# First FFN of a two-layer encoder step: parts of x shared between the opening's plain products and the seven operands, and the first chunk's down products by seven

## The chip, the cores and the metric

The kernel runs on one core of a Trainium2 chip. The engines of the core work in parallel and are tied together by semaphores: PE (matmul), DVE (vector work), ACT (scalar-engine copies and functions), POOL, and SP, which issues loads. The metric is the device time of one execution in microseconds; before the change the median of three runs is 2510.49 us (2510.39 to 2510.75). In this text "width" is the number of elements per partition: 128x320 is 128 partitions of 320.

## The reference

One inference step of an encoder trunk with two layers, 640 tokens in all (512 of a prompt, 8 times 16 of running streams), model width 1024, inner FFN width 2816, all in fp32.

```python
for l in range(DEPTH):                                  # DEPTH = 2
    x = x + 0.5 * _swiglu(_rmsnorm(x, norm_ffn1[l]), w_ffn1_gu[l], w_ffn1_down[l])
    x = x + mixer(_rmsnorm(x, norm_mix[l]))             # short conv + band attention, gated
    x = x + 0.5 * _swiglu(_rmsnorm(x, norm_ffn2[l]), w_ffn2_gu[l], w_ffn2_down[l])
y = _rmsnorm(x, norm_final)

def _swiglu(h, w_gu, w_down):
    g, u = jnp.split(h @ w_gu, 2, axis=-1)
    return (jax.nn.silu(g) * u) @ w_down
```

(Shortened: the reference carries prompt and streams separately and returns keys, values and convolution states too.) The change lies in the first FFN of the first layer.

## The kernel before, in words

**Layout.** x is held transposed: eight tiles x[0..7] of 128 model columns by T = 640 tokens. A block of a weight matrix is 128x128. Tokens are cut into two halves t1 and t2 of HT = 320, since one matmul writes 320 wide.

**Three matmuls for one product.** Every operand is split into a high part (fp32r, the copy on ACT) and a low part (the rest, a subtraction on DVE, `split`, `flush`, `low`). A product of weight w and operand x is wh·xh + wh·xl + wl·xh: three matmuls for each half of the tokens. Weights arrive in raw slabs of 128x1024 (eight blocks), loaded by SP, and are split by `prep` (ACT, line 320) and `flush` (DVE, line 325) into whi and wlo, three buffers each.

**Plain and by seven.** A plain product (`multiply`, `product`) goes over both halves of the tokens: for two blocks of rows of the weight, two of x and two halves of tokens that is eight block products. By seven (`gate_up`, `down_rows`) the same 2x2x2 is done with seven block products, whose operands are sums: of the weights four (X's partners 65, 6, ... built on DVE by `source` from the raw slabs with `add`, line 264) and of x or of the activations also four. In the code the seven operands of x are named X11, X21, X22, XT5, XN6, XT7, XT4; E holds the even tile's sums, O the odd one's. The name `ex.ops[kp]` is a pair of tiles (hi, lo) of seven parts each, for x's tiles 2kp and 2kp + 1. Four partial sums a, b, c are kept in PSUM and copied out by ACT in between (c1, u2, c5; lines 779 to 798 and 832 to 848), since PE goes on adding into the same bank: PE's next product into a bank waits for the copy.

**The FFN** (`ffn`) takes its 22 blocks of inner width in chunks, for the first FFN 4, 4, 4, 4, 4, 2. For a chunk it makes gate and up products (`gate_up`, by seven, one call for each block), and between them the down products of the chunk before: plain, "down", two of x's tiles at a time with `pd` as PSUM tile; or by seven, "rows", four tiles at a time (`down_rows`, PSUM tiles `d..`), which `by_seven` decides. In a rows block DVE adds four of the partial sums for each two tiles straight into x (`take`, line 991), and ACT's copies of the others are added by transfers that POOL issues (`send`, line 986). `Pair` makes the seven operands of two activations for the latter, `later` and `TURNS` say at which places of the following work its sums are made.

**The opening** (`opening`) is the first chunk of the first FFN. x is not normalised yet, so its four gates and ups are made plainly from x times the norm's gain, product after product (PSUM tiles `po`, 0 to 7) with slab i for product i, while x's squares, the norm and then, by `ex.final`, the seven operands of x for later chunks are made between. The scale of the norm, rho, is multiplied in afterwards. At its end the four activations u are split by `parts`, run as `tails` in the first `gate_up` that follows (branch `first`, block 4). The four plain down pieces of this chunk follow gate/ups 4, 5, 6 and 7.

**Order.** In this stretch the order on PE, DVE and ACT is the one in which the code records the work (`ORDERED`); from block 6 on (`free`) only PE's is, and the others are placed by a scheduler.

```python
def by_seven(name, j):
    at, n = chunk_at(name, j)
    return n == 4 and at >= FFNS[name][1] and at + n < FT
```

FFNS["a0"][1] is 4, the number of blocks of the opening.

Of the kernel before, what the change touches and what calls it, by code (L numbers as in the profile page):

```python
# [22 lines left out]
T = SEQ + NB * TS  # L23
HT = T // 2
# [6 lines left out]
KT = D // P  # L31
FT = FF // P
# [8 lines left out]
NP = KT // 2  # L41
# [18 lines left out]
XT4, XN6, XT7, X21, X22, X11, XT5 = range(7)  # L60
# [123 lines left out]
def halves(t):  # L184
    return t.rearrange("p (a b) -> p a b", a=2)
# [3 lines left out]
def trunk(ctx: ExitStack, tc: tile.TileContext, xin, wst, small, pbias, samplebias, kcache, vcache,  # L189
# [36 lines left out]
    def split(hi, lo, src):  # L226
        ACT.copy(hi, src)
        DVE.tensor_tensor(out=lo, in0=src, in1=hi.bitcast(F32), op=ALU.subtract)
# [31 lines left out]
            SP.dma_start(raw, wst[n])  # L260
        return raws[i]

    def add(out, a, b):
        DVE.tensor_tensor(out=out, in0=a, in1=b, op=ALU.add)  # L264

    h1, h2 = slice(0, CH // 2), slice(CH // 2, CH)
    whole = slice(0, CH)
# [55 lines left out]
    def flush():  # L323
        for lo, src, hi in pending:
            DVE.tensor_tensor(out=lo, in0=src, in1=hi.bitcast(F32), op=ALU.subtract)  # L325
        pending.clear()
# [20 lines left out]
    def begin():  # L347

        prep(used[0] + 2)
# [33 lines left out]
    def multiply(ps, ws, xs, first, last):  # L383
        (wh, wl), (xh, xl) = ws, xs
        for j, (w, x) in enumerate(((wh, xh), (wh, xl), (wl, xh))):
            for a in range(2):
                PE.matmul(ps[:, a, :HT], w, x[:, a * HT : (a + 1) * HT],  # L387
                          start=first and j == 0, stop=last and j == 2)

    def steps(ps, ops, at=()):  # L390
# [32 lines left out]
    POOL.memset(epst, EPS)  # L423
    early = cp.tile([P, 1], F32, name="early")

    less = cp.tile([P, L * KT], F32, name="less")
    POOL.tensor_scalar(out=less, in0=sm[:, O_GM : O_GM + L * KT], scalar1=-1.0, scalar2=None, op0=ALU.mult)

    x = [xp.tile([P, T], F32, name=f"x{k}") for k in range(KT)]
    for k in range(KT):  # L430
# [73 lines left out]
    class Expand(Stats):  # L504
# [12 lines left out]
        def final(self, m, square=True):  # L517
# [46 lines left out]
            elif not end:  # L564
                self.add()

        def flush(self):
            for lo, src, hi in self.late:
                DVE.tensor_tensor(out=lo, in0=src, in1=hi.bitcast(F32), op=ALU.subtract)
            self.late.clear()  # L570
# [42 lines left out]
            ACT.activation(early, epst, AF.Silu)  # L613
            self.known = True

    def opening(fp, name, goff, n, put, tails):

        ACT.copy(early, epst)  # L620
        ex = Expand(fp, name, goff)
        h = []
        whi, wlo = (wp.tile([P, CH], F32R, tag=f"w{t}", name=f"w{t}0", bufs=3) for t in ("hi", "lo"))
        ready.append((whi, wlo))
        for k in range(KT):
            g = sm[:, goff + k : goff + k + 1]
            hi = hp.tile([P, T], F32R, tag="hhi", name=f"hhi{name}_{k}")
            lo = hp.tile([P, T], F32R, tag="hlo", name=f"hlo{name}_{k}")
            ACT.activation(hi, x[k], AF.Copy, scale=g)
            c = slice(k * P, (k + 2) * P)  # L630
            if k % 2 == 0:
                ACT.copy(whi[:, c], raws[0][:, c])
            DVE.scalar_tensor_tensor(out=lo, in0=x[k], scalar=g, in1=hi.bitcast(F32),
                                     op0=ALU.mult, op1=ALU.subtract)
            if k % 2 == 0:
                DVE.tensor_tensor(out=wlo[:, c], in0=raws[0][:, c], in1=whi[:, c].bitcast(F32),
                                  op=ALU.subtract)
            h.append((hi, lo))
        flush()

        made = {2: (0, 1), 3: (2, 3), 4: (4,), 5: (5, 6), 6: (7,)}
        us, gs, ps = [], [], []

        def out(i):

            j, up = divmod(i, 2)
            if not up:
                gs.append(tmp(f"g{name}_{j}"))
                if j:
                    scaled(gs[j], ps[i], ex.rho)  # L650
                    ACT.activation(gs[j], gs[j], AF.Silu)
                else:
                    ACT.copy(halves(gs[j]), two(ps[i]))
                return
            u = tmp(f"u{name}_{j}") if j > 1 else fp.tile([P, T], F32, tag="cap", name=f"u{name}_{j}", bufs=5)
            us.append(u)
            if j:
                scaled(u, ps[i], ex.rho)
                DVE.tensor_tensor(out=u, in0=u, in1=gs[j], op=ALU.mult)
# [36 lines left out]
        ahead()  # L696
        begin()
        out(2 * n - 1)

        def parts(j, u):  # L700
            hi = hp.tile([P, T], F32R, tag="hhi", name=f"ahi{name}_{j}")
            lo = hp.tile([P, T], F32R, tag="hlo", name=f"alo{name}_{j}")
            split(hi, lo, u)
            put(j, (hi, lo))
# [179 lines left out]
    class Pair:  # L884
# [8 lines left out]
        def product(self, n, u, g, hi, lo):  # L893
# [15 lines left out]
            self.low(halves(lo), halves(hi), z[:, at])  # L909
            self.keep(kinds, hi, lo)  # L910

        def low(self, lo, hi, z):
            DVE.tensor_tensor(out=lo, in0=z, in1=hi.bitcast(F32), op=ALU.subtract)

# [116 lines left out]
    def ffn(name, fp, ex, goff, after, end=False):  # L1031
# [7 lines left out]
        hold[0] = True  # L1039

        mode = ExitStack()
        free = min(j for j in range(FT) if by_seven(name, j)) + 2

        def order(engines):
            mode.close()
# [1 line left out]

        order(ORDERED)
        if plain:
            ex = opening(fp, name, goff, plain, act.__setitem__, tails)  # L1050
# [166 lines left out]
    class Operands:  # L1217
# [21 lines left out]
        def minus(self, out, a, s, b):  # L1239
            DVE.scalar_tensor_tensor(out=out, in0=a, scalar=s, in1=b, op0=ALU.mult, op1=ALU.subtract)  # L1240
# [665 lines left out]
```

## Time and profile before

| | |
|---|---|
| median of 3 runs | 2510.49 us |
| span of the profiled execution | 2509.0 us |
| instructions | 43304 |
| share of busy time | PE 99%, DVE 85%, ACT 53%, POOL 10% |
| opening, PE's plain products | to 67.2 us from the start |
| gate/up and plain down of blocks 4 to 7 | 67.2 to 144.9 us |
| granted TensorE clock, mean | 0.999 |

The profile is one execution on the chip. Its span is from the first to the last instruction, 1.49 us under the median of the runs, which are timed as a whole. A row of the time-ordered views is start, length, engine, line, operation, what it writes and what it reads; in brackets stands the idle time before it and what ended that. In the chain of waits each piece is what the next one had to wait for. Groups and rows name tiles without their buffer numbers, so paa is tile `pa` of an FFN "a".

### The profile page before, as it was taken

How to read it: one execution, taken by the hardware profiler on the slowest of the kernel's cores; microseconds unless marked ns; L12 is line 12 of the kernel's file. 1: busy time of each engine (PE TensorE's matmuls, PEld its weight loads, DVE VectorE, ACT ScalarE, POOL GpSimd, SP SyncE). 2: the span in 40 equal slices, each digit the busy share in tenths (PEclk: the TensorE clock that was granted, in tenths of full speed). 3: DMA queues.
4: the chain of work that ended last, by engine and by line, in shares of the span. 5: the costliest groups of instructions: out<-in, count | busy, mean ns of one | idle time of the engine just before them, and what ended most of it. 6: DMA issues, size and time to landing. Idle time of an engine off the chain costs nothing.

```text
span 2509.0 us, 43304 instructions
## 1 busy us (share of the span) xinstructions
PE 2492.6 (99%) x17192; PEld 2442.1 (97%) x17192; DVE 2127.7 (85%) x3443; ACT 1322.0 (53%) x2068; POOL 254.0 (10%) x377
## 2 busy tenths in 40 slices
PE   9999999999999999999999999999999999999998
PEld 8999999889999999999999999998899999999998
DVE  7889998888777899998699999988786768899997
ACT  7445556664444545555455555556644455455553
POOL 0001112112000001100001111121210000011111
PEclk9999999999999999999999999999999999999999
DMA  4233445334222234443224443443442222244534
GB/s 145 76 100 103 122 116 127 108 121 156 76 88 93 73 102 116 109 107 100 84 74 111 110 120 104 115 118 117 140 137 85 76 94 76 87 114 109 119 102 102
DMA packets 101003, 265.43 MB, mean 106 GB/s; under 512 B 11360, under 2 KB 46816, under 8 KB 100800
## 3 DMA queue, kind: packets, MB, share of 16 engines
q1 hardware_dynamic: 69408, 220.76, 27.8%
q0 software_dynamic: 30528, 41.26, 9.2%
q8 instruction: 135, 2.21, 0.4%
q10 hardware_dynamic: 864, 0.65, 0.1%
q14 instruction: 68, 0.56, 0.1%
HBM read 222.70 MB, written 7.94 MB: 92 GB/s over the span
## 4 chain that ended last, share of the span: by engine, by line
PE 96%; DVE 2%; issue 1%; ACT 1%; DMA 1%; SPq 0%; DVEq 0%; ACTq 0%; POOLq 0%
PE pab L410 12%; PE paa L410 11%; PE pcb L410 6%; PE pca L410 6%; PE daa L964 5%; PE py L387 4%; PE po L387 4%; PE qa L410 4%; PE dab L964 4%; PE pdb L387 4%; PE pbb L410 3%; PE pba L410 3%; PE dca L964 3%; PE ma_cv L410 2%; PE ma_qk L410 2%; PE pda L387 2%
## 5 line engine op out<-in xcount | busy, mean ns | idle before, releaser
L320 ACT CAST whi<-raw 128x1024 fp32r<-128x1024 f32 (+1 forms) x566 | 509.5, 904 | 392.9 <-PE pba L410 37.2
L325 DVE TENSOR_TENSOR wlo<-raw,whi 128x1024 fp32r<-128x1024 f32 (+1 forms) x566 | 585.6, 1037 | 139.1 <-ACT whi L320 136.8
L320 ACT CAST whi<-s 128x1024 fp32r<-128x1024 f32 (+1 forms) x152 | 144.4, 950 | 266.6 <-issue 91.6
L410 PE MATMUL pab<-xhib,whi 128*128 128x320 f32 x704 | 218.3, 310 | 0.3
L410 PE MATMUL pab<-xlob,whi 128*128 128x320 f32 x704 | 217.4, 309 | 0.0
L410 PE MATMUL pab<-xhib,wlo 128*128 128x320 f32 x704 | 217.4, 309 | 0.0
L410 PE MATMUL paa<-xhia,whi 128*128 128x320 f32 x640 | 198.1, 309 | 1.0 <-ACT c_a L845 0.7
L410 PE MATMUL paa<-xhia,wlo 128*128 128x320 f32 x640 | 197.5, 309 | 0.0
L410 PE MATMUL paa<-xloa,whi 128*128 128x320 f32 x640 | 197.5, 309 | 0.0
L325 DVE TENSOR_TENSOR wlo<-s,whi 128x1024 fp32r<-128x1024 f32 (+1 forms) x152 | 166.1, 1093 | 5.5 <-ACT whi L320 5.5
L986 POOL DMA_DIRECT2D x<-c_b x56 | 49.3, 1023 | 1067.1 <-DVE x L991 783.6
L986 POOL DMA_DIRECT2D x<-c_a x72 | 63.5, 1024 | 834.0 <-ACT whi L320 510.6
L410 PEld LDWEIGHTS pab<-xhib,whi 128*128 128x128 f32 x704 | 132.2, 188 | 0.9 <-ACT c_b L845 0.8
L410 PEld LDWEIGHTS pab<-xlob,whi 128*128 128x128 f32 x704 | 132.2, 188 | 0.2
L410 PEld LDWEIGHTS pab<-xhib,wlo 128*128 128x128 f32 x704 | 132.2, 188 | 0.0
L410 PEld LDWEIGHTS paa<-xhia,whi 128*128 128x128 f32 x640 | 120.1, 188 | 1.6 <-ACT c_a L845 0.9
L410 PEld LDWEIGHTS paa<-xloa,whi 128*128 128x128 f32 x640 | 120.1, 188 | 0.1
L410 PEld LDWEIGHTS paa<-xhia,wlo 128*128 128x128 f32 x640 | 120.1, 188 | 0.0
L410 PE MATMUL pcb<-xhib,wlo 128*128 128x320 f32 x352 | 108.9, 309 | 0.0
L410 PE MATMUL pcb<-xhib,whi 128*128 128x320 f32 x352 | 108.7, 309 | 0.0
L410 PE MATMUL pcb<-xlob,whi 128*128 128x320 f32 x352 | 108.7, 309 | 0.0
L264 DVE TENSOR_TENSOR raw<-raw,raw 128x512 f32<-128x512 f32 x152 | 103.8, 683 | 0.5
(683 smaller groups left out, 7992.8 us busy)
## 6 DMA issues: line engine op xcount, KB each, us to landing
raw<-in_wst SPq DMA_DIRECT2D x378, 512.0 KB, 3.6
x<-c_a POOLq DMA_DIRECT2D x72, 160.0 KB, 4.5
x<-c_b POOLq DMA_DIRECT2D x56, 160.0 KB, 3.4
kc<-in_kcache SPq DMA_DIRECT2D x32, 256.0 KB, 3.6
vc<-in_vcache SPq DMA_DIRECT2D x16, 512.0 KB, 4.6
x<-u_a POOLq DMA_DIRECT2D x36, 160.0 KB, 4.3
x<-u_b POOLq DMA_DIRECT2D x28, 160.0 KB, 4.1
bias<-in_pbias POOLq DMA_DIRECT2D x16, 256.0 KB, 3.7
```

Source lines behind the costliest of these rows:

```text
L264: DVE.tensor_tensor(out=out, in0=a, in1=b, op=ALU.add)
L320: ACT.copy(hi[:, d], src[:, c])
L325: DVE.tensor_tensor(out=lo, in0=src, in1=hi.bitcast(F32), op=ALU.subtract)
L387: PE.matmul(ps[:, a, :HT], w, x[:, a * HT : (a + 1) * HT], start=first and j == 0, stop=last and j == 2)
L410: PE.matmul(ps, a, b, start=start and kp == 0 and j == 0, stop=stop and kp == NP - 1 and j == 2, skip_group_check=True)
L964: PE.matmul(ps[u], w, y, start=start and i == 0 and j == 0, stop=i == 1 and j == 2, skip_group_check=True)
L986: POOL.dma_start(x[ms[2 * u + r]][:, cols], z[:, u], accum_op=ALU.add)
```

## The change

The opening's operands of x are now written into the places that the seven operands keep. For a pair of x tiles `Expand.plain` makes the even one's first half at X11 of `ex.ops[kp]`, its second half in a side tile (two 320-wide instructions on ACT, two on DVE, where one each stood), and the odd one's halves at X21 and X22, at once. `multiply` takes such an operand as a pair of halves. `Expand.mixed` later makes only what is missing: T5 (from the even tile), then N6, T4 and T7.

The first chunk's down products go by seven: `by_seven` no longer leaves the opening's chunk out, so its four plain pieces become two "rows" blocks, one after gate/up 5 and one after 6. That also takes two sets of four slabs where four plain slabs stood, from as many raw loads. The operands of the two pairs of activations are made by hand in the opening, by the new `Pair.even`, `odd` and `mixed`: pair 0's even ones in product 4's place, its odd and mixed ones after product 7, pair 1's even ones behind them, its odd and mixed ones as tails in gate/up 4.

```diff
@@ by_seven
-    return n == 4 and at >= FFNS[name][1] and at + n < FT
+    return n == 4 and at + n < FT
@@ multiply
-                PE.matmul(ps[:, a, :HT], w, x[:, a * HT : (a + 1) * HT],
+                PE.matmul(ps[:, a, :HT], w, x[a] if isinstance(x, tuple) else x[:, a * HT : (a + 1) * HT],
@@ class Expand
+        def plain(self, m):
...
+            if odd:
+                hi, lo = (z[:, 3:5] for z in self.ops[kp])
+                ACT.activation(hi, halves(x[m]), AF.Copy, scale=g)
+                low(lo, halves(x[m]), hi)
+                return tuple(tuple(z[:, a] for a in range(2)) for z in (hi, lo))
...
+            out = (hi[:, X11], self.side[0][:, c]), (lo[:, X11], self.side[1][:, c])
+            for a, (h, l) in enumerate(zip(*out)):
+                src = x[m][:, a * HT : (a + 1) * HT]
+                ACT.activation(h, src, AF.Copy, scale=g)
+                low(l, src, h)
+            return out
+
+        def mixed(self, kp):
...
+            ACT.activation(E[:, 2], e2, AF.Copy, scale=ge)
+            minus(E[:, 1], e1, ge, E[:, 2])
+            self.flush()
+            ACT.copy(hi[:, XT5], E[:, 1])
+            self.late.append((lo[:, XT5], E[:, 1], hi[:, XT5]))
+            yield
+            self.flush()
+            O = self.fp.tile([P, 5, HT], F32, name=f"xo{n}", tag="odd", bufs=1)
+            minus(O[:, XN6], o2, no, E[:, 1])
+            minus(O[:, XT4], o1, no, O[:, XN6])
+            minus(O[:, XT7], o2, go, E[:, 2])
+            ACT.copy(hi[:, 0:3], O[:, 0:3])
+            self.late.append((lo[:, 0:3], O[:, 0:3], hi[:, 0:3]))
+            yield
@@ opening
             for m in made.get(i, ()):
-                ex.final(m, False)
+                next(mixed[m])
             if i == 3:
                 DVE.tensor_tensor(out=u, in0=u, in1=g, op=ALU.mult)
+            if i == 4:
+                pairs[0].even(us[0])
             if i == max(made):
-                ex.rest()
+                ex.flush()
         ahead()
         begin()
+        pairs[0].odd(us[1])
+        pairs[0].mixed()
         out(2 * n - 1)
-        def parts(j, u):
...
-        for j in sorted(range(n), key=lambda j: j < 2):
-            tails.append(lambda j=j: parts(j, us[j]))
+        pairs[1].even(us[2])
+        tails += [lambda: pairs[1].odd(us[3]), lambda: None, pairs[1].mixed]
@@ class Pair
+        def even(self, u):
...
+            add(self.A[:, 0], u[:, :HT], u[:, HT:], ALU.subtract)
+            for a, z in enumerate((u[:, :HT], self.A[:, 0])):
+                ACT.copy(halves(hi)[:, a], z)
+                self.low(halves(lo)[:, a], halves(hi)[:, a], z)
+            self.keep((X11, XT5), hi, lo)
+
+        def odd(self, u):
...
+            ACT.copy(hi, u)
+            for out, a, b in ((B[:, 0], A[:, 0], u[:, HT:]), (A[:, 1], B[:, 0], u[:, :HT])):
+                DVE.scalar_tensor_tensor(out=out, in0=a, scalar=-1.0, in1=b, op0=ALU.mult, op1=ALU.subtract)
+            add(B[:, 1], u[:, HT:], self.u0[:, HT:], ALU.subtract)
+            self.low(lo, hi, u)
+            self.keep((X21, X22), hi, lo)
+
+        def mixed(self):
...
+            ACT.copy(halves(hi), self.B)
+            self.low(halves(lo), halves(hi), self.B)
+            self.keep((XN6, XT7), hi, lo)
...
+            ACT.copy(hi, self.A[:, 1])
+            self.low(lo, hi, self.A[:, 1])
+            self.keep((XT4,), hi, lo)
```

More of the change, by code (lines that the diff above doesn't have):

```diff
@@ L261, in load, with add @@
         return raws[i]
-    def add(out, a, b):
-        DVE.tensor_tensor(out=out, in0=a, in1=b, op=ALU.add)
+    def add(out, a, b, op=ALU.add):
+        DVE.tensor_tensor(out=out, in0=a, in1=b, op=op)
     h1, h2 = slice(0, CH // 2), slice(CH // 2, CH)
@@ L424, in trunk @@
     early = cp.tile([P, 1], F32, name="early")
-    less = cp.tile([P, L * KT], F32, name="less")
-    POOL.tensor_scalar(out=less, in0=sm[:, O_GM : O_GM + L * KT], scalar1=-1.0, scalar2=None, op0=ALU.mult)
+    less, less1 = (cp.tile([P, n * KT], F32, name=f"less{n}") for n in (L, 1))
+    for z, o in ((less, O_GM), (less1, O_G1)):
+        POOL.tensor_scalar(out=z, in0=sm[:, o : o + z.shape[1]], scalar1=-1.0, scalar2=None, op0=ALU.mult)
     x = [xp.tile([P, T], F32, name=f"x{k}") for k in range(KT)]
@@ new lines, in mixed, with minus @@
+        def mixed(self, kp):
+            n = f"{self.name}_{kp}"
+            hi, lo = self.ops[kp]
+            (e1, e2), (o1, o2) = ([x[2 * kp + i][:, c] for c in (slice(0, HT), slice(HT, T))] for i in range(2))
+            ge, go = (sm[:, self.goff + 2 * kp + i :][:, 0:1] for i in range(2))
+            no = less1[:, 2 * kp + 1 : 2 * kp + 2]
+            E = self.fp.tile([P, 3, HT], F32, name=f"xe{n}", tag="even", bufs=1)
+            def minus(out, a, g, b):
+                DVE.scalar_tensor_tensor(out=out, in0=a, scalar=g, in1=b, op0=ALU.mult, op1=ALU.subtract)
+            ACT.activation(E[:, 2], e2, AF.Copy, scale=ge)
[12 more added lines that the diff above has]
+            yield
@@ L614, in spread, with opening @@
             self.known = True
-    def opening(fp, name, goff, n, put, tails):
+    def opening(fp, name, goff, n, pairs, tails):
         ACT.copy(early, epst)
@@ L625, in opening @@
         for k in range(KT):
[L626 to L629, printed above, removed]
+            h.append(ex.plain(k))
             c = slice(k * P, (k + 2) * P)
@@ L632, in opening @@
                 ACT.copy(whi[:, c], raws[0][:, c])
-            DVE.scalar_tensor_tensor(out=lo, in0=x[k], scalar=g, in1=hi.bitcast(F32),
-                                     op0=ALU.mult, op1=ALU.subtract)
-            if k % 2 == 0:
                 DVE.tensor_tensor(out=wlo[:, c], in0=raws[0][:, c], in1=whi[:, c].bitcast(F32),
                                   op=ALU.subtract)
-            h.append((hi, lo))
         flush()
+        mixed = [z for kp in range(NP) for z in [ex.mixed(kp)] * 2]
         made = {2: (0, 1), 3: (2, 3), 4: (4,), 5: (5, 6), 6: (7,)}
@@ L690, in opening @@
             for m in made.get(i, ()):
-                ex.final(m, False)
+                next(mixed[m])
             if i == 3:
                 DVE.tensor_tensor(out=u, in0=u, in1=g, op=ALU.mult)
+            if i == 4:
+                pairs[0].even(us[0])
             if i == max(made):
-                ex.rest()
+                ex.flush()
         ahead()
         begin()
+        pairs[0].odd(us[1])
+        pairs[0].mixed()
         out(2 * n - 1)
-        def parts(j, u):
[L701 to L704, printed above, removed]
-        for j in sorted(range(n), key=lambda j: j < 2):
-            tails.append(lambda j=j: parts(j, us[j]))
+        pairs[1].even(us[2])
+        tails += [lambda: pairs[1].odd(us[3]), lambda: None, pairs[1].mixed]
         ex.rest = None
@@ L1041, in ffn @@
         mode = ExitStack()
-        free = min(j for j in range(FT) if by_seven(name, j)) + 2
+        free = max(plain, min(j for j in range(FT) if by_seven(name, j))) + 2
         def order(engines):
@@ L1049, in ffn @@
         if plain:
-            ex = opening(fp, name, goff, plain, act.__setitem__, tails)
+            for i, j in enumerate(range(0, plain, 2)):
+                pairs[j] = Pair(fp, f"{name}_{j}", i, later, None)
+            ex = opening(fp, name, goff, plain, [pairs[j] for j in range(0, plain, 2)], tails)
         for what, a in ffn_order(name):
```

20 lines of the change are left out of this document (added).

## The prediction

> **What bounds the kernel now.** I read the page first: the busy times and the chain that ended last. Then PE's list of waits, then the chain, DVE and ACT in order of time over the first 170 us, the only stretch in which the order of instructions changes: in the built program DVE, ACT and PE differ in their first rows alone, SP's row is the same throughout, and POOL has 13 instructions more.
>
> ```profile
> span 2509.0 us, 43304 instructions
> PE 2492.6 (99%) x17192; PEld 2442.1 (97%) x17192; DVE 2127.7 (85%) x3443; ACT 1322.0 (53%) x2068; POOL 254.0 (10%) x377
> PE 96%; DVE 2%; issue 1%; ACT 1%; DMA 1%; SPq 0%; DVEq 0%; ACTq 0%; POOLq 0%
> ```
>
> PE is the bound: 96% of the chain. So a matmul that goes away is worth its pitch, and work on DVE and ACT is free until PE has to wait for it. How rarely it does so now:
>
> ```profile
> PE poa L387 <- ACT whi L632: 5.6, 1, 5.6
> ...
> PE paa L410 <- ACT c_a L845: 0.7, 1, 0.7
> PE poa L387 <- DVE wlo L325: 0.4, 1, 0.4
> ...
> PE paa L410 <- ACT c_a L832: 0.3, 1, 0.3
> ```
>
> The columns are total, count and longest. 5.6 us is the start of the kernel, 0.4 the second weight slab. The two on c_a are PE waiting until ACT has copied a partial sum out of PSUM, at the head of layer 2's first FFN; they come back below.
>
> **The saving.** The chain in order of time (start, length, what):
>
> ```profile
> 14.99 1.24 DVE wlo L325
> ...
> 16.27 10.23 PE poa L387 x68
> ...
> 79.74 7.04 PE pda L387 x48
> ...
> 169.53 1.76 PE daa L964 x12
> ```
>
> 48 plain down matmuls take 7.04 us, 12 of the seven-product kind 1.76: both 0.147 us each. The first chunk's plain down is 4 x 48 = 192 matmuls, 28.16 us. By seven it is two blocks of seven products of 12 matmuls, 2 x 7 x 1.76 = 24.64 us. **Term 1: -3.52 us**, 24 matmuls. The opening's own products keep their number and shape; only where their operand lies changes, so 0.
>
> **The start.** The chain runs through the second slab's arrival and split until 16.27. Each even part of x is now made by two 320-wide instructions on ACT and two on DVE instead of one each.
>
> ```profile
> 10.60 1.67 ACT L629 ACTIVATE hhia<-x,sm 128x640 fp32r<-128x640 f32 x2 [0.46 <-DMA x<-in_xin]
> ...
> 13.90 1.05 ACT L320 CAST whi<-raw 128x1024 fp32r<-128x1024 f32 x1 [0.44 <-DMA raw<-in_wst]
> ...
> 69.50 0.42 ACT L779 COPY c_a<-paa 128x320 f32<-128x320 f32 x1
> ```
>
> ACT waits for x's sixth part before 10.60 and for the slab before 13.90. Between the two lies one even part: half width costs between half of 0.83 and all of it, so 0 to 0.83 more; a 320-wide copy takes 0.42 (69.50), which puts the pair near 0.9, 0.1 more. The 0.44 of idle time covers it. **Term 2: 0**; uncovered, up to 0.4.
>
> **The opening's DVE work.** DVE rows (start, length; in brackets the idle time before):
>
> ```profile
> 36.14 0.82 DVE L502 TENSOR_TENSOR ga<-poa,rhoa 128x640 f32<-128x640 f32 x1 [1.92 <-ACT rhoa L611]
> ...
> 52.26 0.49 DVE L547 SCALAR_TENSOR_TENSOR xoa<-xoa 128x320 f32<-128x320 f32 x1
> ...
> 53.08 0.82 DVE L569 TENSOR_TENSOR xloa<-xoa,xhia 128x640 fp32r<-128x640 f32 x1
> ...
> 67.78 0.69 DVE L264 TENSOR_TENSOR raw<-s,raw 128x512 f32<-128x512 f32 x1
> 68.38 0.82 DVE L502 TENSOR_TENSOR ua<-poa,rhoa 128x640 f32<-128x640 f32 x1
> 69.30 0.83 DVE L659 TENSOR_TENSOR ua<-ua,ga 128x640 f32<-128x640 f32 x1
> 70.04 1.22 DVE L325 TENSOR_TENSOR wlo<-raw,whi 128x1024 fp32r<-128x1024 f32 x1
> 71.18 1.55 DVE L228 TENSOR_TENSOR aloa<-ua,ahia 128x640 fp32r<-128x640 f32 x2
> ```
>
> Per pair of x the low part of the odd one (0.82) goes and that of the even one shrinks from 640 to 320 wide (0.82 to 0.49): 1.15 less. Pair 0's share only lengthens the wait of 1.92 before 36.14. Pairs 1 to 3 give 3.45; the first down pair's even half, new in here, takes one subtraction and two low parts, 1.47. So DVE is up to 2.0 us ahead when it comes to the sum at 67.78: done by 66.5, not 68.47. That is worth nothing by itself, as PE did not wait.
>
> **Where the work goes that was cheap: the first stall.** In the plain down the four activations were just split (the row of 71.18 and its like), half of them behind the third slab. By seven the first pair's odd and mixed operands and the second pair's even ones are made at the end of product 7, and in DVE's and ACT's fixed order they stand ahead of the copy of a partial sum that the first gate/up's PE work waits for.
>
> ```profile
> 67.25 0.31 PE L410 MATMUL paa<-xhia,whi 128*128 128x320 f32 x1
> ...
> 70.78 0.31 PE L410 MATMUL paa<-xhia,whi 128*128 128x320 f32 x1
> ```
>
> ```profile
> 68.55 1.06 ACT L320 CAST whi<-raw 128x1024 fp32r<-128x1024 f32 x1 [1.92 <-DVE raw L264]
> ...
> 69.82 1.36 ACT L227 CAST ahia<-ua 128x640 fp32r<-128x640 f32 x2
> ```
>
> At 70.78 PE adds the next product into the sum that it wrote at 67.25; the copy at 69.50 must have read it. New order on ACT: third slab's cast, odd, mixed, T4, even's first half, even's second half, then that copy. On DVE: three subtractions, three low parts, u of activation 3 (scaled, then times g), even's subtraction. Step by step:
> - The cast takes the buffer that product 7 reads last (three buffers), so it starts at 67.2 and runs 0.97 until the next can start: 68.2. The odd operand's cast, half of 1.36 plus a hand-over, ends at 68.9.
> - DVE's low parts wait for it: 0.74 + 0.74 + 0.41 (a 320-wide one, 0.49 less 0.08 of overlap): 70.8.
> - u of activation 3: 68.38 to 70.04 in the rows, less 0.05 of waiting, 1.6: 72.4. The subtraction, 0.5: 72.9.
> - ACT: even's second half, 0.33, then the copy, 0.42, and the hand-over to PE: 73.75.
>
> PE was ready at 70.78. **Term 3: +3.0 us.** Lower end 0.1: if even's second half did not wait for DVE, ACT alone would have the copy done by 70.9 (68.8 + 0.64 + 3 x 0.33 + 0.42). Upper end 4.2: with no lead on DVE the cast starts at 68.5. I take 3.0, as 66.5 lies well before 67.2.
>
> **The second stall.** Before, one of those 7.04 us pieces of plain down stood between the first gate/up and the second, in which DVE caught up. Now the second follows at once, still in the fixed order. The nearest rows are layer 2's, where the first two gate/ups already stand so:
>
> ```profile
> 1272.50 0.69 DVE L264 TENSOR_TENSOR s<-raw 128x512 f32<-128x512 f32 x1
> ```
>
> ```profile
> 1280.25 0.43 ACT c_a L845
> 1280.72 2.04 PE paa L410 x12
> ```
>
> ```profile
> 78.02 0.49 DVE L264 TENSOR_TENSOR ua<-pca,c_a 128x320 f32<-128x320 f32 x1
> 78.42 1.22 DVE L325 TENSOR_TENSOR wlo<-raw,whi 128x1024 fp32r<-128x1024 f32 x1
> ```
>
> From the first slab sum to PE's product T7 of the second gate/up there are 8.22 us: two sums, a split, two more sums, the gate's product, its difference, ACT's cast, and behind it the copy of u2 (line 845; 890 in the changed kernel). The new chain is the same. From the end T of the product X22 it needs 0.04 + 0.40 + 1.14 (78.02 to the end of 78.42's, less overlap) + 8.22 = 9.8. PE comes there after five products, 5 x 1.76 - 0.17 = 8.6. **Term 4: +1.2 us**; bounds 0.7 (what that place cost in layer 2) and 1.9 (the same again with a split of 0.7 ahead).
>
> **The rest of chunk 1.**
>
> ```profile
> 67.30:168.00 100.70, 100.70 (x688) 100.70 (x687) 84.01 (x123) 44.25 (x64) 0.00 (x0) 1.00 0.26 84
> ```
>
> This row has stretch, PE, PEld, DVE, ACT, POOL. DVE is idle for 16.7 us in it. Added by durations: slabs, 2 x (three full splits of 1.22, a half one and four sums of 0.69) for 4 x 1.22, +9.3; x's updates, 16 x 0.49 for 8 x 0.82, +1.3; down operands, two pairs of four subtractions and three narrow low parts at 0.49 and two wide ones at 0.82, less the 1.47 made earlier, 8.7 for 3.1, +5.6: 16.2, and 13.7 when each of the 31 more (12, 8 and 11) overlaps its neighbour by 0.08. DVE then works 97.7 us of about 102. So small waits of 0.2 to 0.4, like the c_a rows', are due in the two row blocks: **term 5: +0.8** (0 to 1.5). POOL's 12 new transfers into x are waited for only by the next update of the same part, a block later: 0.
>
> **Sum:** -3.52 + 0 + 3.0 + 1.2 + 0.8 = +1.5 us. Nothing after about 240 us changes, and PE bounds it all, so the shift stays: span 2510.5. The median lies 1.49 over this span: **2512.0 us**, +0.06%. A measurement of this kernel can tell about 0.2%, 5 us, from no change.
>
> **Rivals.**
> - *The saving comes through.* The casts and low parts find room as in the later chunks, whose waits in PE's list are 0.3 at most; only the measured 0.7 is left: -2.8, 2507.7. For it: ACT works 44.25 us of 100.70. Against: the copy stands behind DVE, in an order that is written out.
> - *DVE becomes the bound, slower.* Place: between the first gate/up and the second row block; it decides once more than 5 us of DVE's idle time cannot be used. If 9 of the 16.7 us stay idle, the stretch takes 97.7 + 9 = 106.7, 6 more than 100.7: 2516.5. For it: 97.7 of 102 is close. Against: from the third gate/up on only PE's order is fixed, and DVE starts 2 us ahead.
> - *The clock.* A stall of 3 us may cost PE its clock.
>
> ```profile
> 5.58 0.90 PE L387 MATMUL poa<-hhia,whi 128*128 128x320 f32 x2 [5.58 <-ACT whi L632]
> ...
> 7.97 0.74 PE L387 MATMUL poa<-hloa,whi 128*128 128x320 f32 x2
> ...
> 9.36 0.45 PE L387 MATMUL poa<-hloa,whi 128*128 128x320 f32 x2
> ```
>
> ```profile
> 2500.00:2502.00 2.00, 0.60 (x4) 0.52 (x4) 1.97 (x6) 0.68 (x2) 0.00 (x0) 1.00 0.80 283
> 2502.00:2504.00 2.00, 0.70 (x2) 0.30 (x2) 2.00 (x6) 0.00 (x0) 0.00 (x0) 1.00 0.76 273
> 2504.00:2506.00 2.00, 0.00 (x0) 0.00 (x0) 2.00 (x6) 0.00 (x0) 0.00 (x0) 0.56 1.03 346
> ```
>
>   At the start pairs of matmuls run slow for about 3.4 us, 5.58 to 9.0. Paying that once more at half speed costs 1.7: 2513.7. At the end the granted clock (third last column) was still 1.00 some 4 us after the dense work, so 3.0 should not be enough. The Trainium skill (TensorE: Matmul & The Clock Gate, "What's actually happening") has the clock halved after an idle window of about 3.4 us, free-running; by that rule a stall of 3.0 stays just inside and one of 4.2 does not; the trace's end agrees.
> - *The change does less than it says:* the start slips by the 0.4 of term 2, all else as forecast: 2512.4.
>
> **How the numbers follow.** Forecast 0.65, with 2510 to 2514.5 as its own range (terms 3 to 5 between 3.0 and 7.5; their ends add up to 0.8 and 7.6); the saving 0.13; DVE bound 0.12; clock 0.05; start 0.05. The range leaves out the saving's case and most of DVE's, where they lie beyond 2508.8 and 2515.2. Faster by over 0.2% would need more than the 3.52 that there is: 0.02. Slower by over 0.2% (2515.5 on) is most of DVE's case: 0.08. Within: 0.90.
>
> **What would show it.** PE 24 matmuls fewer, at 0.147; the gate/up at 67.25 unmoved to 0.3; a wait of paa on ACT's copy of line 824 near 3.0 and on line 890's near 1.2; the clock 1.00 throughout; DVE over 95% busy until about 165; from 240 us on a constant shift of about +1.5. The prediction is wrong if the first wait is under 1 or over 4.5, if PE waits for wlo in that gate/up, or if the shift grows later.

## The result, and the profile after

| | before | after |
|---|---|---|
| median, measured side by side (20 runs each) | 2510.78 us | 2514.77 us |
| lowest to highest | 2510.39 to 2512.01 | 2514.13 to 2515.82 |
| span of the profiled execution | 2509.0 us | 2513.0 us |
| PE instructions | 17192 | 17168 |

The ratio is 1.0016, with a 95% interval of 1.0011 to 1.0022: slower by 4.0 us, where 1.5 were forecast. That lies inside the range, and just outside the forecast's own (up to 2514.5).

First two lines of the changed kernel's page, then PE's list of waits (total, count, longest):

```profile
span 2513.0 us, 43349 instructions
PE 2492.6 (99%) x17168; PEld 2440.5 (97%) x17168; DVE 2138.2 (85%) x3477; ACT 1323.7 (53%) x2082; POOL 264.6 (11%) x390
```

```profile
PE poa L387 <- ACT whi L684: 5.5, 1, 5.5
PE paa L410 <- ACT c_a L824: 3.5, 1, 3.5
PE paa L410 <- ACT c_a L890: 1.6, 2, 0.9
...
PE paa L410 <- DVE wlo L325: 0.3, 1, 0.3
```

24 matmuls are gone, and yet PE's busy time is the same as before, 2492.6 us. So beside the waits something made matmuls longer. The two stalls of the forecast are there: line 824's, and line 890's, of whose total of 1.6 us 0.9 is here and 0.7 is the old one of layer 2. The chain of waits through the first one, and the granted clock in stretches of 2 us (third last column):

```profile
67.96 1.05 ACT whi L320
69.02 0.63 ACT ohia L973
...
69.67 0.83 DVE oloa L993
70.50 0.73 DVE tloa L993
71.24 0.40 DVE t4loa L993
71.64 0.75 DVE ua L503
...
72.41 0.83 DVE ua L708
73.23 0.41 DVE paa L264
...
74.03 0.43 ACT c_a L824
...
74.51 2.74 PE paa L410 x12
77.25 2.58 PE pba L410 x12
79.83 1.76 PE paa L410 x12
```

```profile
72.00:74.00 2.00, 0.00 (x0) 0.00 (x0) 1.97 (x4) 0.33 (x1) 0.00 (x0) 1.00 0.00 0
74.00:76.00 2.00, 1.49 (x9) 1.50 (x10) 1.88 (x4) 1.41 (x4) 0.00 (x0) 0.88 0.00 0
76.00:78.00 2.00, 2.00 (x9) 2.00 (x9) 1.82 (x4) 0.72 (x2) 0.00 (x0) 0.50 0.58 133
78.00:80.00 2.00, 2.00 (x13) 2.00 (x12) 0.14 (x1) 1.49 (x4) 0.00 (x0) 0.76 0.32 129
80.00:82.00 2.00, 2.00 (x15) 2.00 (x15) 2.00 (x4) 0.77 (x1) 0.00 (x0) 1.00 0.00 0
```

The chain is the one that the forecast wrote down, link for link, but it begins at 67.96, not 67.2. And after the wait the clock falls to half. In the three stretches 0.12, 0.50 and 0.24 of the clock is missing; where it is halved, 0.50 is missing, so it was halved for 2 x (0.12 + 0.50 + 0.24) / 0.50 = 3.4 us. Two blocks of 12 matmuls take 2.74 and 2.58 us there, and the next 1.76 again. Below, such a stretch at half speed is called a dip.

PE's rows at the two stalls, and at the wait for a weight's low part (wlo) of the list, which stands in the third gate/up:

```profile
74.51 0.42 PE L410 MATMUL paa<-xhia,whi 128*128 128x320 f32 x1 [3.54 <-ACT c_a L824]
...
93.20 0.41 PE L410 MATMUL paa<-xhia,whi 128*128 128x320 f32 x1 [0.91 <-ACT c_a L890]
...
115.39 0.42 PE L410 MATMUL paa<-xhia,wlo 128*128 128x320 f32 x1 [0.27 <-DVE wlo L325]
```

Where the 4.0 us come from, added up over PE's rows of this stretch (what lies between the starts of two matmuls beyond 0.147 us; each stop adds some 0.27 there to the wait in the bracket): the first stall 3.8; the clock 1.5; the second stall 1.2; small losses behind these 0.85 (0.1 near 88.7, 0.2 near 102.2, 0.5 near 115.4); the saving -3.52. That is +3.8. At 243.46 before, 247.38 after, PE starts the same row block ("daa"): a shift of 3.92, which then stays.

### The profile page after: what moved, and what is told of

Read it like the earlier page. It is cut to its first block, busy times and chain, and to the rows that moved or that the text cites. A ratio compares the mean times of both kernels' runs of the same rounds, so it can differ in the third digit from the quotient of the medians.

```text
span 2513.0 us, 43349 instructions
## 1 busy us (share of the span) xinstructions
PE 2492.6 (99%) x17168; PEld 2440.5 (97%) x17168; DVE 2138.2 (85%) x3477; ACT 1323.7 (53%) x2082; POOL 264.6 (11%) x390
## 4 chain that ended last, share of the span: by engine, by line
PE 93%; DVE 4%; ACT 1%; issue 1%; DMA 1%; SPq 0%; DVEq 0%; ACTq 0%; POOLq 0%
PE pab L410 12%; PE paa L410 11%; PE pcb L410 6%; PE pca L410 5%; PE daa L1044 5%; PE py L387 4%; PE po L387 4%; PE qa L410 4%; PE dab L1044 4%; PE pdb L387 4%; PE pbb L410 3%; PE dca L1044 3%; PE pba L410 3%; PE ma_cv L410 2%; PE ma_qk L410 2%; PE pv L1487 2%
## 5 line engine op out<-in xcount | busy, mean ns | idle before, releaser
L320 ACT CAST whi<-raw 128x1024 fp32r<-128x1024 f32 (+2 forms) x568 | 510.6, 902 | 384.1 <-PE pbb L410 38.9
L325 DVE TENSOR_TENSOR wlo<-raw,whi 128x1024 fp32r<-128x1024 f32 (+2 forms) x568 | 586.6, 1036 | 135.5 <-ACT whi L320 132.9
L1066 POOL DMA_DIRECT2D x<-c_a x80 | 70.4, 1031 | 826.9 <-ACT whi L320 372.5
```

Source lines behind the costliest of these rows:

```text
L320: ACT.copy(hi[:, d], src[:, c])
L1066: POOL.dma_start(x[ms[2 * u + r]][:, cols], z[:, u], accum_op=ALU.add)
```

## The experiments

Three questions: is the shared place of x's parts free, as the forecast has it; why was the first stall longer than 3.0; and what moved the clock. All times are medians beside runs of the kernel before on the same chip (2510.7 to 2510.8).

### e1: the first half of the change alone

The new places of x's parts, with the first chunk's down products plain as before:

```diff
 def by_seven(name, j):
     at, n = chunk_at(name, j)
-    return n == 4 and at + n < FT
+    return n == 4 and at >= FFNS[name][1] and at + n < FT
```

(`opening` splits the four activations with `parts`, as before.)

> The first half of the change alone: x's parts are made once and kept, the first chunk's down products stay plain. Theory (the loss comes from the down operands that stand in DVE's and ACT's order ahead of PSUM copies): PE does the 17192 matmuls of before, waits nowhere new in the first 170 us, and the time is that of before within 0.5 us (about 2510.8), although DVE does some 4 us less in the opening: what DVE saves there is hidden under PE. Rival (the parts' new places or the start cost something by themselves): 0.5 to 2 us slower than before, with a wait before the first gate/up.

2510.71 us, ratio 0.9999 (0.9990 to 1.0008). PE has no new wait. The first half costs nothing and brings nothing; terms 1 and 3 to 5 all come with the down products. These alone, with the old opening, weren't tried: x's old operands fill the buffers that the new ones need.

### e5, e6, e7: a wait of a chosen length in the kernel before

Idle copies on ACT ahead of the first copy of a partial sum; 3, 4 and 8 of them. Nothing else changes, so the whole difference is what such a wait costs at that place.

```diff
             mul(pa, s0, 0, X11, every, True, True)
+            if not new:
+                for _ in range(4):
+                    ACT.copy(ex.ssum, x[0])
             ACT.copy(c1, pa)
```

> The kernel before, with three idle copies of x[0] (640 wide, 0.74 us from one to the next on ACT) into a finished sum, put ahead of the first copy out of PSUM in the gate/up of block 4. That copy then ends at about 72.1 instead of 69.9, and PE waits 1.4 us at a place where nothing else changed. Theory W (the granted clock is decided in fixed windows of 3.41 us, the length of the two dips recorded so far, and falls for the next window when well over half of one was idle): 1.4 of 3.41 is 41%, no dip, +1.4 us. Rival (any wait over 1 us costs the clock): a dip of 3.4 us at 0.50, +3.1 us.

> The same with four idle copies: PE waits 2.1 us, as long as in the run with pair 1's even operands ahead of u, where the clock dipped. Theory W: with the window where it falls in that run the idle share is over 60%, and a dip costs 1.7 us more; where the wait is split between two windows (up to 1.1 and 1.0) there is none, so the executions differ among themselves, between +2.1 and +3.8 us. Rival (a whole window of 3.4 us must be idle): +2.1 in all of them, clock 1.00.

> The same with eight idle copies: PE waits 5.2 us. Theory W: at least one window is mostly idle in every execution, but the dip may begin while PE still waits, so that part of it costs nothing: one dip or two, +5.2 and between 0.5 and 2.5 us more, 2516.5 to 2518.5. Rival (the dip's price does not depend on where it begins): +6.9 us in each.

| | wait in PE's rows | time lost, profiled | clock at half | median | runs |
|---|---|---|---|---|---|
| e5 | 1.19 us | 1.5 us | no | +1.6 us | 2511.45 to 2513.01 |
| e6 | 1.94 us | 2.2 us | not in the profiled run | +3.6 us | 2512.84 to 2513.09 (4), 2514.29 to 2515.39 (6) |
| e7 | 4.97 us | 7.6 us | yes | +7.8 us | 2517.73 to 2519.78 |

e5's short wait costs itself and the 0.26 us of the stop, and no more. e6's runs fall into two groups with nothing between them; the profiled one, 2513.07, belongs to the lower group and lost its wait and the stop (1.94 + 0.26). The upper group's median, 2515.0, is 2.0 above the lower's. The mean granted clock, which is on record for every run, is 0.999 in the four and 0.998 in the six. So a wait of 1.94 us costs the clock in some executions and not in others. Both dips cost more than the 1.7 us that was expected: e6's slowest run is at +4.7, not +3.8, and e7's median lies at the end of its band. e7 shows the dip in its rows:

```profile
75.54 0.64 PE L410 MATMUL paa<-xhia,whi 128*128 128x320 f32 x1 [4.97 <-ACT c_a L782]
```

```profile
72.00:74.00 2.00, 0.00 (x0) 0.00 (x0) 0.00 (x0) 1.91 (x4) 0.00 (x0) 1.00 0.66 252
74.00:76.00 2.00, 0.46 (x2) 0.46 (x3) 0.00 (x0) 1.97 (x4) 0.00 (x0) 0.52 0.00 0
76.00:78.00 2.00, 2.00 (x9) 2.00 (x9) 1.56 (x2) 1.07 (x3) 0.00 (x0) 0.50 0.00 0
78.00:80.00 2.00, 2.00 (x10) 2.00 (x9) 0.00 (x0) 0.85 (x2) 0.00 (x0) 0.50 0.00 0
80.00:82.00 2.00, 2.00 (x12) 2.00 (x12) 0.23 (x1) 1.72 (x4) 0.00 (x0) 0.77 0.00 0
```

Here the clock falls at 74.1, in the middle of the wait, 3.5 us after PE stopped, and comes back at 80.9: 6.8 us, twice the 3.4 of the changed kernel.

### e9: the lead that was lost

The last low part that the opening makes for x stands behind the next slab's sums.

```diff
+            if i == 2 * n - 1:
+                ex.flush()
             flush()
             for m in made.get(i, ()):
                 next(mixed[m])
...
-            if i == max(made):
-                ex.flush()
```

> The changed kernel with one instruction moved: x's last low part of the opening (960 wide), which lets DVE wait 1.06 us for ACT's cast at 61.76, stands behind the next slab's two sums and the gate's scaling. Theory L (DVE's lead was lost in that wait, and the lead sets the first stall): the second raw sum starts near 66.1 where it started at 67.17, the third slab's cast on ACT moves from 67.96 to the 67.2 at which its buffer comes free, and the first wait falls by about 0.75, from 3.5 to 2.8; the total falls by 0.75 if the clock's dip stays and by up to 2.4 if it goes (2512.4 to 2514.0). Rival (the stall is set by the chain behind the cast alone, or by product 7): the wait stays within 0.2 of 3.5 and the total at 2514.8.

DVE's row before the move (the changed kernel), and ACT's and PE's after it (e9):

```profile
61.76 1.16 DVE L624 TENSOR_TENSOR xloa<-xoa,xhia 128x960 fp32r<-128x960 f32 x1 [1.06 <-ACT xhia L618]
...
67.17 0.69 DVE L264 TENSOR_TENSOR raw<-s,raw 128x512 f32<-128x512 f32 x1
```

```profile
65.48 0.68 DVE L264 TENSOR_TENSOR raw<-s,raw 128x512 f32<-128x512 f32 x1
```

```profile
67.25 1.05 ACT L320 CAST whi<-raw 128x1024 fp32r<-128x1024 f32 x1 [3.44 <-PE poa L387]
...
73.31 0.42 ACT L824 COPY c_a<-paa 128x320 f32<-128x320 f32 x1
```

```profile
73.78 0.41 PE L410 MATMUL paa<-xhia,whi 128*128 128x320 f32 x1 [2.80 <-ACT c_a L824]
```

With the sum at 65.48 the cast no longer waits for DVE but for PE, as the bracket says, at 67.25; and from there the chain runs to 73.78, where the forecast had 73.75. The wait falls from 3.5 to 2.8. Theory L holds: the stall was longer than forecast by the lead that DVE did not have. (The sum came earlier than expected, 65.48 and not 66.1; 0.44 of that is DVE's wait for the weight's cast ahead of 65.42, which fell away too. Nothing is gained by it, as the buffer comes free at 67.2.) The median is 2513.76, 1.0 under the changed kernel; the profiled execution, at 2512.42 the shortest of 11, has no dip, and the longest is 2515.13. So a wait of 2.8 us seems to cost the clock in many executions still, but no trace of one of the longer executions was kept.

### e2 and e10: the copy does not wait for u

The second pair's even half is made ahead of u of activation 3, so the copy that PE waits for stands behind two DVE instructions less. e10 adds e9's move.

```diff
         pairs[0].mixed()
-        out(2 * n - 1)
         pairs[1].even(us[2])
+        out(2 * n - 1)
```

> The changed kernel with one order changed: pair 1's even operands are made ahead of activation 3's u (two DVE instructions, 1.6 us together) instead of behind it. The first copy out of PSUM in the gate/up of block 4 should come 1.6 us earlier, so PE's wait there shrinks from 3.7 to about 2.1 us. Theory with the clock (the wait of 3.7 is what halves the granted clock for 3.4 us): at 2.1 the clock stays at 1.00, and 1.7 us come on top of what the waits save; some of the 1.6 comes back as waits of 0.5 further on, so 2.3 to 3.3 us faster than the changed kernel, about 2512. Rival (the clock falls for another reason, such as the load of that place): the dip stays and the gain is 0.9 to 1.6 us, about 2513.5.

> That move and, as in e2, the second pair's even half ahead of u of activation 3. Theory L with the clock: the two gains add, 1.6 and 0.75, so the first wait is 1.1 to 1.2, too short for a dip in any execution; with the other two waits as they were (1.1 and 0.4 to 0.5) the total is -3.52 + 1.2 + 1.2 + 0.8 = -0.3 beside the kernel before, 2510.4 (2510.0 to 2511.2), and its runs spread by less than those of e2. Rival: the wait stays near the 1.9 of e2, the dip stays in part of the executions, and the total is 2512.9.

e2: the wait is 1.93 us, near the 2.1 expected, the median 2512.95 (2511.66 to 2514.37). Here too there are two groups: five runs up to 2512.16, all with a mean clock of 0.999, and six from 2512.95 on, all with 0.998. The profiled execution is one of the six, and its clock fell:

```profile
73.53 0.42 PE L410 MATMUL paa<-xhia,whi 128*128 128x320 f32 x1 [1.93 <-ACT c_a L824]
```

```profile
72.00:74.00 2.00, 0.47 (x3) 0.47 (x4) 1.88 (x5) 0.78 (x2) 0.00 (x0) 1.00 0.00 0
74.00:76.00 2.00, 2.00 (x11) 2.00 (x10) 1.97 (x3) 0.69 (x2) 0.00 (x0) 0.60 0.00 0
76.00:78.00 2.00, 2.00 (x10) 2.00 (x9) 1.97 (x5) 1.02 (x4) 0.00 (x0) 0.54 0.24 61
```

That is the same wait as e6's 1.94 us, once with the dip and once without.

e10: the wait is 1.21, the clock 1.00 throughout, the median 2511.45, ratio 1.0003 (0.9994 to 1.0011). The two gains add, as theory L has it. It is 0.25 above the end of the expected band: there is a new wait of 0.32 on DVE's "ga" at 79.70, which the expectation left out. PE's rows add up to +0.6 beside the saving (1.5, 0.55, 0.1, 1.2 and 0.8, less 3.52), the medians to +0.8.

### e3: everything behind the copy

The even half behind the first copy of a partial sum, the odd and mixed operands behind the third:

```diff
-        pairs[1].even(us[2])
-        tails += [lambda: pairs[1].odd(us[3]), lambda: None, pairs[1].mixed]
+        tails += [lambda: pairs[1].even(us[2]), lambda: None, lambda: pairs[1].odd(us[3]), pairs[1].mixed]
```

> The changed kernel with pair 1's even operands made behind the first copy out of PSUM in the gate/up of block 4, and its odd operand behind the third, so that nothing stands before that copy but pair 0's casts. Theory A (a matter of one place in ACT's queue): the wait of 3.7 us goes to about 0.2, nothing takes its place, and with the clock kept the time is some 5 us under the changed kernel's, about 2509.5, faster than before. Theory B (DVE has more to do in that stage than PE gives it time for): the first wait goes, but 2 to 3 us of new waits stand further on in the same gate/up, on the third slab's low part or the next copies; no single one over 3, so the clock is kept: 2 to 3 us under the changed kernel's, about 2512.

2512.37 us, ratio 1.0005 (0.9996 to 1.0014), 2.4 under the changed kernel. The first wait is gone (0.3 us are left of it), but behind it stand two new ones of 1.4 and 1.2 us in PE's rows, on the copy of line 842 and on DVE's "ga". No dip. Of the 3.8 us only 0.9 went away: in this order too the copies waited for DVE's work. The rest of the gain is the clock's.

### e4: the low parts on POOL

The subtractions of the two opening pairs on POOL, which has nothing to do here:

```diff
         def low(self, lo, hi, z):
-            DVE.tensor_tensor(out=lo, in0=z, in1=hi.bitcast(F32), op=ALU.subtract)
+            (DVE if self.spots else POOL).tensor_tensor(out=lo, in0=z, in1=hi.bitcast(F32), op=ALU.subtract)
```

> The changed kernel with the ten low parts of the first chunk's two operand pairs (subtractions of 320 or 640 wide, about 6 us of DVE in all) made by POOL instead of DVE; the order is the same. Theory B (DVE's load sets the waits): the first wait falls from 3.7 to about 1 us, the clock is kept, and the time comes to about 2510.2, near or under that of before. Rival (POOL is too slow, or slows DVE by working beside it): the operands are late for the first row block, where PE then waits for them, or DVE's rows in that stage grow longer; the time stays over 2512.

2515.84 us, ratio 1.0020 (1.0011 to 1.0029): 1.1 more than the changed kernel. The first wait is 3.4 us. DVE's and POOL's rows say why:

```profile
69.50 1.95 DVE L708 TENSOR_TENSOR ua<-ua,ga 128x640 f32<-128x640 f32 x1
71.38 1.81 DVE L264 TENSOR_TENSOR paa<-ua 128x320 f32<-128x320 f32 x1
73.12 1.88 DVE L325 TENSOR_TENSOR wlo<-raw,whi 128x1024 fp32r<-128x1024 f32 x1
```

```profile
69.20 1.58 POOL L993 TENSOR_TENSOR oloa<-ua,ohia 128x640 fp32r<-128x640 f32 x1 [19.86 <-ACT ohia L973]
70.73 2.11 POOL L993 TENSOR_TENSOR tloa<-pba,thia 128x640 fp32r<-128x640 f32 x1
72.81 1.10 POOL L993 TENSOR_TENSOR t4loa<-paa,t4hia 128x320 fp32r<-128x320 f32 x1
```

The same instructions take 0.83, 0.48 and 1.22 us on DVE when POOL computes nothing. So DVE, though spared the low parts, came no earlier: its own instructions grew longer while POOL worked beside it. PE's rows lose as much in this stretch as in the changed kernel, and the profiled execution, at 2514.66 the shortest of 11, is no longer than that kernel's; what the others have more, 1.1 us at the median, no trace shows.

### e11, e8 and e12: the written order, and a better one

e11 lets the scheduler place DVE's and ACT's work from the gate/up of block 5 on. e8 does so from block 4, and in the opening puts the first pair's odd and mixed operands two products earlier, in product 5's place; the second pair's stand as in e3. e12 is e8 with e9's move.

```diff
@@ e11
-        free = max(plain, min(j for j in range(FT) if by_seven(name, j))) + 2
+        free = max(plain, min(j for j in range(FT) if by_seven(name, j))) + (1 if plain else 2)
@@ e8
+            if i == 5:
+                pairs[0].odd(us[1])
+                pairs[0].mixed()
...
-        pairs[0].odd(us[1])
-        pairs[0].mixed()
...
+        free = max(plain, min(j for j in range(FT) if by_seven(name, j))) + (0 if plain else 2)
```

> The changed kernel with only PE's order fixed from the gate/up of block 5 on (one block earlier), so a scheduler places DVE's and ACT's work there. Theory (terms 4 and 5 come from the written order of DVE and ACT, terms 3 and the clock from the block before): first wait 3.5 and the dip stay, the waits behind it of 1.2 and 0.8 fall to 0.5 to 1 together, total about 1.1 under the changed kernel, 2513.6. Rival (those waits are DVE's load, whatever the order): total within 0.4 of 2514.8.

> The changed kernel with three moves: pair 0's odd and mixed operands are made at product 5 instead of after product 7; pair 1's even ones behind the first copy out of PSUM in the gate/up of block 4 and its odd ones behind the third; and only PE's order is fixed from block 4 on (two blocks earlier), so that a scheduler places DVE's and ACT's work. Theory B (the waits come from DVE's work being too dense there in a fixed order, and the copies wait in line behind it): the waits of 3.7, 1.2 and 0.8 us become several of 0.4 to 1.0, together 2.5 us or less, none long enough to cost the clock: 1 us under the kernel before, about 2509.8, and 5 under the changed one. Rival (DVE's amount alone decides, and the order only moves the waits): together still 4 us or more, 2511.5 or slower.

> e8 with e9's move: x's last low part of the opening stands behind the next slab's two sums and the gate's scaling, so DVE does not sit out the 1.07 us of ACT's cast at 65.07. Theory (in e8 too that lost time comes back as PE's waits): the waits of 0.86 for the weight's low part and about 0.6 behind it shrink by 0.7 to 1.4 together, total about 1 under e8, 2509.2 (2508.7 to 2509.8), which would be 1.5 under the kernel before. Rival (the scheduler's new order spends it elsewhere): total within 0.4 of e8's 2510.2.

e11: 2514.10 us, 0.7 under the changed kernel and not the 1.1 expected. In the profiled execution the losses behind the first gate/up fall from 2.05 to 0.9 us, which is the 1.1; but the clock is at half there for 6.8 us, not 3.4, and takes 2.3 instead of 1.5. The waits answer to the theory; the medians alone, with the clock in them, would not have settled it.

```profile
74.10 3.57 PE paa L410 x12
77.67 2.58 PE pba L410 x12
80.25 1.76 PE paa L410 x12
```

e8: 2510.20, ratio 0.9997 (0.9988 to 1.0006). The waits in this stretch are 0.70 on a weight's low part and 0.46 on "ga", then smaller ones; no dip. e12: **2508.36 us, ratio 0.9990 (0.9981 to 0.9999)**, 2.4 us under the kernel before and 6.4 under the changed one. Its waits on copies and low parts:

```profile
...
PE paa L410 <- ACT c_a L890: 0.7, 1, 0.7
PE pca L410 <- ACT c_a L893: 0.6, 3, 0.2
PE po L387 <- DVE m_6lo L228: 0.4, 2, 0.2
PE paa L410 <- ACT c_a L877: 0.3, 1, 0.3
```

The 0.7 on line 890 is layer 2's old one. In this stretch PE's rows lose 0.8 us of the 3.52, which leaves 2.7; 2.4 were measured, 0.3 better than the expected band. The move that took 0.7 us of wait away in e9 was worth 1.8 here: e8's waits on the weight's low part and on "ga" are both gone. The interval ends just under one, so that it beats the kernel before is likely and its size uncertain.

## Why the prediction was right or wrong

The path was right, and that the change loses. Two steps failed, both in the same direction: the size of the first stall, which still lay within its bounds (0.1 to 4.2), and the clock, which was no term of the sum. That the time lies in the range all the same is partly luck.

- **Term 1, the saving (-3.52): right.** 24 PE instructions fewer, each at 0.147 us; e12 has most of it in its time.
- **Term 2, the start (0): right.** The first gate/up starts at 67.28, where it was 67.25, and e1 is at 0.9999. (Between the profiled executions of this study that start lies anywhere from 66.8 to 67.9, so e1's medians are the better evidence.)
- **Term 3, the first stall (+3.0): its path was right, its size wrong; measured 3.8.** The step that failed is "DVE is up to 2.0 us ahead when it comes to the sum at 67.78: done by 66.5". It was 0.6 ahead: the sum started at 67.17. The low part that fell away had stood where DVE would otherwise have waited for ACT's cast of 960:

```profile
61.22 0.82 DVE L569 TENSOR_TENSOR xloa<-xoa,xhia 128x640 fp32r<-128x640 f32 x1
62.37 1.16 DVE L569 TENSOR_TENSOR xloa<-xoa,xhia 128x960 fp32r<-128x960 f32 x1 [0.33 <-ACT xhia L554]
```

  These are the kernel before's rows: 0.33 us of waiting behind 0.82 of work. After, 1.06 of waiting stand there (the row of 61.76). From the first low part of this pair to the slab's sum DVE took 4.29 us before (59.16 to 63.45) and 4.14 after (58.69 to 62.83): 0.15 saved, where the forecast counted 1.15 for each pair. A second, smaller part: the subtraction that multiplies by x's gain, a value for each partition, takes 0.55 us at 320 wide, where its like without the gain took 0.49. e9 gave the lead back, and the rest of the term was right to 0.03 us.
- **Term 4, the second stall (+1.2): right.** 1.2 in PE's rows, 0.91 of it in the list of waits.
- **Term 5, the rest (+0.8): the size right, the places not, so partly luck.** 0.85 were lost, but the two row blocks, where the waits were forecast, have only 0.2 of it (near 102.2); 0.5 is the third gate/up's wait for a weight's low part. DVE did 96.1 us of work from 67.3 to 171.9, where PE begins the same work as at 168.0 before; 97.7 were forecast. That is 92% of the stretch, not over 95%.
- **The clock: the rival came true beside the forecast, +1.5, which had been given a chance of 0.05.** The step that failed is "so 3.0 should not be enough". It was drawn from the end of the trace, where the clock was 1.00 "some 4 us after the dense work"; but PE still worked 0.60 and 0.70 of 2 us there, so this was no full wait. (For the same reason the prediction's "the trace's end agrees" does not hold: in the 3.41 us ahead of the fall, at 2504.23, PE was busy for 0.97.) And a dip was treated as something that a wait has or doesn't have. e6 and e2 show waits of the same length without and with it. The price, 1.7 by half speed for 3.4 us, was near: 0.267 us between matmuls instead of 0.147 loses 1.5.
- **The rival "DVE becomes the bound"** named the right engine and the wrong place: 5.0 of the 5.85 us of waiting lay in the first and second gate/up, 3.8 of them ahead of where that rival looked. "The saving comes through" holds for e12's order, not for this one.

With 0.8 more for term 3 and 1.5 for the clock the sum is +3.8, for the +4.0 measured.

## What to carry to other kernels

Work that is taken off an engine makes it earlier only if it did not stand in front of a wait: look at the idle time in the brackets of the next rows before counting a removed instruction as a lead. Where a written order puts work ahead of the copy that the bounding engine waits for, price the wait link by link, and then add the clock: here a wait of 1.2 us cost itself, and one of 1.9 us or more cost some 1.5 to 2.5 us on top in many executions. When a change loses what it should save, move one instruction at a time; here e12's changes of order together turned +4.0 into -2.4 us with the same arithmetic.

## What the hardware showed that was not expected

**Between dense matmuls the clock goes by the idle share of a stretch, not by the length of a wait.** In finer stretches the clock's edges lie at 75.54 and 78.95 in the changed kernel, 3.41 us apart; at 74.41 and 77.82 in e2; 6.83 apart, twice that, in e7 and e11. In the 3.41 us ahead of each fall PE was idle for 2.38 us (70%) in the changed kernel, 1.93 (57%) in e2, 1.95 (57%) in e11 (72.54 less 70.59, the end of its last matmul), 2.15 (63%) in e4 and all of it in e7. With waits of 1.21 us or less, 35% of such a stretch, no profiled execution shows a dip.

These stretches run on by themselves. From the end of the changed kernel's dip, 78.95, to the clock's next fall, 2505.82 at the end of the trace, there are 2426.87 us, 711 times 3.4133. So it depends on the execution whether a wait falls into one stretch or is cut in two. e9 shows a cut. Its matmuls come to full speed near 10.8 us, and its clock falls at 2502.50; counted in steps of 3.4133 from either, an edge lies at 72.2, within the wait of 2.80:

```profile
68.80:72.21 3.41, 2.18 (x15) 1.92 (x14) 3.22 (x5) 1.48 (x4) 0.00 (x0) 1.00 0.00 0
72.21:75.62 3.41, 1.84 (x12) 1.84 (x13) 3.25 (x7) 1.74 (x4) 0.00 (x0) 1.00 0.00 0
```

PE is idle for 1.23 (36%) and 1.57 us (46%), and the clock stays at 1.00. In e6's profiled execution the wait of 1.94 is cut in the same way, into 1.00 and 0.94. So for these matmuls the bound lies between 46% and 57%. If it lay at one half (an estimate), a wait of 1.94 would lose the clock in 1.94 / 3.41 = 57% of executions, and 6 of e6's 10 and 6 of e2's 11 lie in the upper group; one of 2.8 in 82%, and one of 3.5 in all, as the changed kernel's 20 runs within 1.7 us suggest. (These too fall into two groups, 11 up to 2514.78 and 9 from 2515.25 on. A second stretch at half speed would do that, as in e11, but no trace of a run in the upper group was kept.)

Two things stay open. e7 and e11 stayed at half through a second stretch that was 43% and 46% idle, while e9's 46% did not lower a full clock. And at the trace's end idle time in the rows is no guide: in e9 the clock falls at 2502.50 after a stretch with 0.71 us of it (21%). Part of that stretch is filled by matmuls of one column, whose rows are 0.5 to 0.6 us long for four of them, so what exactly is counted was not settled.

The Trainium skill (TensorE: Matmul & The Clock Gate, "What's actually happening") has the clock halved after an idle window of 3.4 us that runs freely, and the length and the free running agree with these edges. That the window must be idle does not: 57% were enough.

**POOL's subtractions slow DVE's.** In e4 DVE's 320-wide subtraction went from 0.48 to 1.81 us and the 640-wide product from 0.83 to 1.95 while POOL subtracted. The Trainium skill (SBUF — State Buffer, "SBUF: two separate sides") has the two engines share a pair of ports that one holds for a whole instruction, also for a DVE instruction with two inputs in SBUF; these rows agree.
